# A hybrid encoder layer on one core: gate-times-up blocks turned by VectorE in squares of 32 and moved across partitions by ScalarE, in place of TensorE's transposes; one seven-product pair fewer in each second chunk

## The chip, the cores and the metric

One core of a Trainium2 chip runs the whole layer in one launch. The metric is the device time in microseconds (us), the median of three runs. All engines, queues and times below are those of this one core.

## The reference

Only the two SwiGLU half-steps are touched, the first and the last stage of the layer (the stages between, projections and three branches, are unchanged):

```python
def rmsnorm(x, g):
    y = xf * lax.rsqrt(jnp.mean(xf * xf, axis=-1, keepdims=True) + EPS)
    return y * g

def swiglu(x, w_gate, w_up, w_down):
    return (jax.nn.silu(x @ w_gate) * (x @ w_up)) @ w_down

x = x + 0.5 * swiglu(rmsnorm(x, ffn1_norm), ffn1_w_gate, ffn1_w_up, ffn1_w_down)
...
x = x + 0.5 * swiglu(rmsnorm(x, ffn2_norm), ffn2_w_gate, ffn2_w_up, ffn2_w_down)
```

x has 256 tokens and 2048 columns, the hidden width is 5632, all in float32.

## The kernel before

**Precision.** Every large product is made of three matmuls. An operand is split into a high part (rounded to the type fp32r, by ScalarE) and a low part (what is left, by VectorE): `wh` and `wl` for weights, `lhs[:, 0]` and `lhs[:, 1]` for the left side. The three matmuls are low times high, high times high, and high times low (`product` in `pair_gemm`, and the same in `gemm` and `down_pieces`).

**Tiling of a half-step.** The hidden width is cut into 11 chunks of 512 columns (`HID`). Chunk c computes gate and up together (`pair_gemm`), in 8 steps, the pairs j: each takes two blocks of 128 rows of the input width, for 2 halves of the tokens (t = 0, 1) and the two matrices. A pair is a 2x2 by 2x2 block product and is made either with eight products (24 matmuls of 128x512) or, after Strassen and Winograd, with seven (21 matmuls). A seven-product pair also needs sums of weight blocks: VectorE adds them (`sums`), ScalarE and VectorE split them (`sumsh`, `sumsl`), beside the split of three of the four own blocks (`wh`, `wl` 128x1536). An eight-product pair needs the split of four blocks (128x2048) and nothing else. `SEVEN` holds the pairs that have seven-product operands on the left side, six of eight. Chunk 0 takes no seven-product pair, chunk 1 of the first half-step takes pairs 2, 4 and 6 (`SEVEN[1::2]`), all others take six.

**After a chunk.** The products gather in eight PSUM banks and end in two tiles in SBUF, gate and up, of 128 partitions (tokens) by 2 by 512. They come from a pool of four (`tmp`) and are called `gate`, `up` or, where they are the second set of the chunk, `late_gate`, `late_up`. ScalarE applies silu to the gate, VectorE multiplies (`product` in `up(c)`, a SCALAR_TENSOR_TENSOR on `late_up`). The result is needed turned, with hidden columns on the partitions, as the left operand of the down product. `turned_lhs` does that with TensorE: 8 transposes of 128x128 per chunk (matmuls `bank<-ident,late_up`) into two PSUM banks, and from each bank a split by ScalarE and VectorE (`lhs<-bank`) into the operand `hT[c]`. They are queued as `turns` and run after the last seven-product pair of the next chunk (`after_seven`).

**Down.** The down product of chunk c is cut into 8 pieces of 12 matmuls and spread between the products of chunk c+2 (`down_pieces`, `between`). Each piece ends with a ScalarE copy `y<-down` and a DMA from GpSimd's queue that adds y to x in DRAM. The last two chunks' down products come at the end of the half-step, in `gemm`.

**What sets the order.** All instructions are recorded first. `Plan.issue` then plays them through with assumed costs and writes out one fixed order for each engine: an engine takes, among the instructions whose inputs are there, the one recorded first; `shifted(n)` lets an instruction count as recorded n places later. `queue` and `pop` spread small work between the products. Weights, sums, splits and left operands share 23 places (`slot`) of 8 KB per partition; a weight's DMA waits until a place is free.

Of the kernel before, what the change touches and what calls it, by code (L numbers as in the profile page):

```python
# [13 lines left out]
AF = mybir.ActivationFunctionType  # L14
# [3 lines left out]
P = 128  # L18
S = 256
T = S // P  # L20
# [22 lines left out]
SEVEN = (1, 2, 3, 4, 5, 6)  # L43
SUMS = (220, 400)
HID = DFF // CW
MIXV = (0, 3)
APART = 4
BETWEEN = 4
# [133 lines left out]
class Plan:  # L182
# [36 lines left out]
    def record(self, engine, name, args, kw):  # L219
        values = list(args) + [v for k, v in kw.items() if k not in ("out", "accum_out")]  # L220
        out = kw.get("out")
        if out is None:
            out, values = args[0], values[1:]
        views = [v for v in values if isinstance(v, View)]
        outs = [v for v in (out, kw.get("accum_out")) if isinstance(v, View)]

        def call():
            real = lambda v: v.real() if isinstance(v, View) else v
            return getattr(getattr(self.nc, engine), name)(*map(real, args), **{k: real(v) for k, v in kw.items()})  # L229

        w = Work(engine, call, *self.cost(engine, name, out, views, kw))
        if name == "dma_start":
            side = out if isinstance(out, View) else views[0]
            w.bytes, w.adds = 4 * P * side.free(), "accum_op" in kw
        w.link = LINKS.get(getattr(kw.get("func", args[2] if name == "activation" else None), "name", None), 0)
        before, tiles = set(), {}
        for view, writes in [(v, False) for v in views] + [(v, True) for v in outs]:
            t, bits = view.tile, view.bits()
            tiles[id(t)] = t
            for other, theirs, wrote in t.log:  # L240
                chained = engine == other.engine == "tensor"
                if other is not w and (theirs & bits and (writes or wrote) or chained and writes and wrote):
                    before.add(other)
            if writes:
                t.log = [x for x in t.log if x[1] & ~bits]
            t.log.append((w, bits, writes))
        w.tiles = tuple(tiles.values())
        for t in w.tiles:
            if t.users == 0:
                t.group.tiles.append(t)  # L250
                t.turn = len(self.works) + self.shift
            t.users += 1
        w.waits = len(before)
        for b in before:
            b.then.append(w)
        w.index = len(self.works) + self.shift
        self.works.append(w)
# [159 lines left out]
def tile_encoder_layer(ctx: ExitStack, tc: tile.TileContext, a: dict, out: bass.AP):  # L417
    nc = Plan(tc)
# [15 lines left out]
    def lslot():  # L434
        return slot([P, 2, 4, S], F32R, "lhs")
# [82 lines left out]
    pending = set()  # L518

    def queue(*work, soon=False):  # L520

        later.extend((f, soon) for f in work)
# [253 lines left out]
    def turned_lhs(src, among, gain=None):  # L776
# [14 lines left out]

        return L, [f for half in range(2) for f in turn_steps(src, half, among, then(half))]

    def turned_pairs(places, n, src, gain):

        pieces = []
        turned = {}

        def by_squares(i):
            if i == 0:  # L800
                turned["y"] = tmp([P, 4, S], "turned")
            turn_pieces(turned["y"], src)[i]()

        pieces += [lambda i=i: by_squares(i) for i in range(4)]
        for half in range(2):
            place = places[2 * n + half]
            pending.add(id(place))
            g = gain[:, 2 * half : 2 * half + 2]
            pieces += fill_pair(place, lambda half=half: turned["y"][:, 2 * half : 2 * half + 2], g)
            pieces.append(lambda place=place: pending.discard(id(place)))  # L810
        return pieces
# [63 lines left out]
    lhs1 = pair_tiles()  # L875
# [4 lines left out]
    def load_x(j):  # L880

        if j % 4 == 0 and j:
            xts.append(slot([P, 8, S], F32, "xt"))
        xt = xts[-1][:, 2 * (j % 4) : 2 * (j % 4) + 2]
        step = 1 if j == 0 else 2
        fill = fill_pair(lhs1[j], lambda: xt, g_ffn1[:, 2 * j : 2 * j + 2], SUMS[j not in SEVEN[1::2]], j == 0)

        def part(k):
            if j or k:
                nc.sync.dma_start(out=xt[:, k : k + step], in_=a["xT"][:, 2 * j + k : 2 * j + k + step, :])  # L890
            for f in fill[:1] if step == 1 else fill:
                f()
            del fill[:1]

        return [lambda k=k: part(k) for k in range(0, 2, step)]
# [24 lines left out]
    def ffn(lhs, rstd, w_gate, w_up, w_down, after_chunk, operand=None, first=None, side=()):  # L920

        hT = {}
        turns, held = [], []

        def second(j):

            if j < 2:
                return [lambda q=q: load_rows(q) for q in (2 * j, 2 * j + 1)]
            if j == 3:
                queue(lambda: rstd.append(rstd_of(ssq1)), *held, soon=True)  # L930
            return ()

        def up(c):

            nonlocal turns
            opening = c == 0 and first is not None
            kw = dict(before=first, pieces=lambda j: 1 if j < 2 else 2) if opening else {}
            if c == 1 and first is not None:
                kw = dict(before=second)
            out = []  # L940
            sevens = () if c == 0 else SEVEN[1::2] if c == 1 and first is not None else SEVEN
            order = [j for j in range(KB // 2) if j not in sevens]
            order = range(KB // 2) if c == 0 or kw else [*sevens, *order]
            between = down_pieces(c - 2) if c > 1 else ()
            pair_gemm(lhs, (w_gate, w_up), (c * CW, c * CW), order, sevens, out, turns, between=between, soon=c == HID - 1, **kw)
            g, u = out
            def silu(t):
                nc.scalar.activation(g[:, t], g[:, t], AF.Silu, scale=rstd[0][:, t : t + 1])

            def product(t):  # L950
                nc.vector.scalar_tensor_tensor(
                    u[:, t], u[:, t], rstd[0][:, t : t + 1], g[:, t], op0=ALU.mult, op1=ALU.mult
                )

            done = [lambda t=t, f=f: f(t) for t in range(T) for f in (silu, product)]
            if opening:
                held.extend(done)
            else:
                queue(*done, soon=True)
            hT[c], turns = turned_lhs(u, (0, 1) if c < HID - 1 else (4, 5))  # L960
            if c == HID - 1:
                queue(*turns)

        def down_pieces(c):

            L = hT.pop(c)
            W = {}

            def piece(n, t):
                if t == 0:  # L970
                    W[n] = weights(w_down, c * CW, n * CW)
                b = psum(7, [P, CW], "down")
                wh, wl = W[n]
                for k in range(4):
                    hi = L[:, 0, k, t * P : (t + 1) * P]
                    lo = L[:, 1, k, t * P : (t + 1) * P]
                    nc.tensor.matmul(b, lo, wh[:, k], start=k == 0, stop=False)
                    nc.tensor.matmul(b, hi, wh[:, k], start=False, stop=False)
                    nc.tensor.matmul(b, hi, wl[:, k], start=False, stop=k == 3)
                y = half_tmp([P, CW], F32, "y")  # L980
                nc.scalar.activation(y, b, AF.Copy, scale=0.5)
                nc.gpsimd.dma_start(out=XD[n][t], in_=y, accum_op=ALU.add)

            return [lambda n=n, t=t: piece(n, t) for n in range(NCH) for t in range(T)]

        for c in range(HID):
            up(c)
        operands = [hT.pop(c) for c in (HID - 2, HID - 1)]
        for n in range(NCH):
            if side:  # L990
                queue(*side[n], soon=True)
            xs = x_chunk(n)
            acc = gemm(operands, w_down, (HID - 2) * CW, n * CW, last=n == NCH - 1 and first is None)

            def residual(t, n=n, acc=acc, xs=xs):
                nc.vector.scalar_tensor_tensor(xs[:, t], acc[t], 0.5, xs[:, t], op0=ALU.mult, op1=ALU.add)
                after_chunk(n, t, xs)

            queue(*(lambda t=t, f=residual: f(t) for t in range(T)), soon=True)
            if operand is not None:  # L1000
                operand(n, xs)
# [566 lines left out]
```

## Time and profile before

| | us |
|---|---|
| median of 3 runs (2264.16 to 2264.96) | 2264.72 |
| the profiled execution, its own time | 2264.33 |
| its span, first to last instruction | 2262.6 |
| first half-step, about | 0 to 700 |
| stages between, about | 700 to 1600 |
| second half-step, about | 1600 to 2262 |

GpSimd is busy for 194.8 us, nearly all of it issuing DMAs. The DMA queues moved 525 MB, 232 GB/s over the span. To read the rows below: a row of the page or of a group gives line, engine and operation, out<-in with buffer numbers left out, shapes and count, then busy time and the mean ns of one, then idle time before them and who ended it. A timeline row gives start, duration, engine, operation and count. Almost every row names line 229, the helper that issues what the planner has ordered, so groups are told apart by tile names. A matmul's duration is longer than the time until the next one starts, since matmuls overlap; what one costs is read from starts.

### The profile page before, as it was taken

What the parts mean: (1) busy time and instruction counts of PE and PEld (TensorE: products, weight loads), DVE (VectorE), ACT (ScalarE), POOL (GpSimd) and SP (SyncE); (2) the same over time, 40 slices, a digit from 0 to 9 for tenths busy, and PEclk for the clock granted to TensorE, in tenths of its full rate; (3) what the DMA queues carried; (4) which work ended last, traced back from release to release, by engine and by line L of the source; (5) the groups of instructions that cost most, each with busy time, mean ns of one, the idle gap of its engine ahead of it and who ended that gap; (6) DMA issues with size and microseconds to landing.
All of it is one profiled execution on the core that took longest, in us unless ns stands there. A gap on an engine that the chain in (4) does not pass through costs nothing.

```text
span 2262.6 us, 26505 instructions
## 1 busy us (share of the span) xinstructions
PE 2252.0 (100%) x10106; PEld 1857.4 (82%) x10106; DVE 1929.6 (85%) x1972; ACT 1305.5 (58%) x1313; POOL 194.8 (9%) x257
## 2 busy tenths in 40 slices
PE   9999999999999999999999999999999999999998
PEld 7888888888888888888888888888888888888887
DVE  7999999999989787757778787899899989999985
ACT  8666666666666454443334454455566666666663
POOL 0011111111110000000000000000011111111110
PEclk9999999999999999999999999999999999999999
DMA  9688899988996555565454556665488898988892
GB/s 372 211 242 252 252 259 264 255 241 249 277 334 217 203 204 168 196 213 197 169 195 174 178 208 230 230 214 211 173 250 240 249 262 246 267 245 244 255 321 115
DMA packets 121584, 525.06 MB, mean 232 GB/s; under 512 B 14320, under 2 KB 14576, under 8 KB 90224
## 3 DMA queue, kind: packets, MB, share of 16 engines
q1 hardware_dynamic: 88848, 444.15, 55.6%
q0 software_dynamic: 32176, 78.66, 17.5%
q8 instruction: 79, 1.29, 0.2%
q10 hardware_dynamic: 432, 0.56, 0.1%
q14 instruction: 49, 0.40, 0.1%
HBM read 458.30 MB, written 46.14 MB: 223 GB/s over the span
## 4 chain that ended last, share of the span: by engine, by line
PE 95%; issue 2%; DMA 1%; DVE 1%; POOL 0%; ACT 0%; SPq 0%; DVEq 0%; POOLq 0%; ACTq 0%
PE acc L229 40%; PE q L229 36%; PE down L229 16%; PE bank L229 2%; DMA x<-y 1%; DMA wf<-in_ffn_w_up 1%; DVE wl L229 0%; POOL x L229 0%; ACT wh L229 0%; SPq L229 0%; DVE sums L229 0%; ACT y L229 0%; POOL late_up L229 0%; POOL late_gate L229 0%; DVE up L229 0%
## 5 line engine op out<-in xcount | busy, mean ns | idle before, releaser
L229 DVE TENSOR_TENSOR wl<-wf,wh 128x2048 fp32r<-128x2048 f32 (+2 forms) x422 | 884.3, 2109 | 106.2 <-ACT wh L229 84.0
L229 ACT ACTIVATE wh<-wf 128x2048 fp32r<-128x2048 f32 (+2 forms) x422 | 741.9, 1769 | 305.3 <-DMA wf<-in_w_in 107.2
L229 PE MATMUL acc<-wh,lhs 128*128 128x512 f32 x2688 | 830.3, 390 | 0.0
L229 PEld LDWEIGHTS acc<-wh,lhs 128*128 128x128 f32 x2688 | 502.5, 188 | 102.6
L229 PE MATMUL acc<-wl,lhs 128*128 128x512 f32 x1344 | 522.7, 389 | 0.0
L229 PE MATMUL down<-wh,lhs 128*128 128x512 f32 x1152 | 357.6, 391 | 0.9 <-ACT y L229 0.8
L229 ACT ACTIVATE sumsh<-sums 128x1024 fp32r<-128x1024 f32 x234 | 244.5, 1058 | 128.7 <-DVE sums L229 123.1
L229 DVE TENSOR_TENSOR sumsl<-sums,sumsh 128x2048 fp32r<-128x2048 f32 x117 | 267.7, 2288 | 45.7 <-ACT sumsh L229 44.7
L229 PEld LDWEIGHTS acc<-wl,lhs 128*128 128x128 f32 x1344 | 252.3, 188 | 52.7
L229 PE MATMUL q<-wh,seven 128*128 128x512 f32 x942 | 292.2, 389 | 0.0
L229 PE MATMUL q<-sumsh,seven 128*128 128x512 f32 x936 | 288.0, 389 | 0.0
L229 PEld LDWEIGHTS down<-wh,lhs 128*128 128x128 f32 x1152 | 215.1, 188 | 48.4 <-ACT y L229 4.6
L229 PE MATMUL q<-wh,lhs 128*128 128x512 f32 x704 | 230.5, 407 | 0.1
L229 PE MATMUL down<-wl,lhs 128*128 128x512 f32 x576 | 224.6, 390 | 0.0
L229 PEld LDWEIGHTS q<-wh,seven 128*128 128x128 f32 x942 | 176.8, 188 | 36.7
L229 PEld LDWEIGHTS q<-sumsh,seven 128*128 128x128 f32 x936 | 175.7, 188 | 36.4
L229 POOL DMA_DIRECT2D x<-y x144 | 123.9, 861 | 808.3 <-ACT y L229 754.7
L229 PE MATMUL q<-wl,seven 128*128 128x512 f32 x471 | 182.9, 389 | 0.2 <-DVE wl L229 0.2
L229 ACT ACTIVATE y<-down 128x512 f32<-128x512 f32 x144 | 86.0, 597 | 161.4 <-PE down L229 127.9
L229 PE MATMUL q<-sumsl,seven 128*128 128x512 f32 x468 | 174.9, 389 | 0.0
L229 DVE TENSOR_TENSOR sums<-sums,wf 128x512 f32<-128x512 f32 x234 | 161.9, 692 | 7.9
L229 PEld LDWEIGHTS q<-wh,lhs 128*128 128x128 f32 x704 | 124.2, 189 | 28.1 <-ACT wh L229 1.1
(149 smaller groups left out, 1667.4 us busy)
## 6 DMA issues: line engine op xcount, KB each, us to landing
wf<-in_w_in SPq DMA_DIRECT2D x100, 1024.0 KB, 4.8
wf<-in_ffn_w_down SPq DMA_DIRECT2D x88, 1024.0 KB, 7.8
wf<-in_ffn_w_gate SPq DMA_DIRECT2D x174, 512.0 KB, 5.7
wf<-in_ffn_w_up SPq DMA_DIRECT2D x174, 512.0 KB, 6.8
x<-y POOLq DMA_DIRECT2D x144, 256.0 KB, 6.9
wf<-in_w_mem_kv SPq DMA_DIRECT2D x16, 1024.0 KB, 6.3
wf<-in_w_out SPq DMA_DIRECT2D x16, 1024.0 KB, 5.4
late_gate<-gate POOLq DMA_DIRECT2D x18, 512.0 KB, 5.5
```

Of the source, the lines that this page charges most:

```text
L229: return getattr(getattr(self.nc, engine), name)(*map(real, args), **{k: real(v) for k, v in kw.items()})
```

## The change

1. In all chunks of both half-steps but the last (10 of 11 each), `turned_lhs` is replaced by `moved_lhs`. VectorE turns the 512 columns of one token half in one instruction on all 128 partitions, in squares of 32x32 (`squares`, 2 per chunk), from up into the gate tile, which silu and product no longer need. A square is turned where it stands, so its partition group stays the token's. ScalarE then moves the squares to the partition group of their columns, from the gate tile back into the up tile, in 16 copies of 32 partitions x 256 (`move`), which the planner counts as recorded 200 places later (`MOVED`). The split into `hT[c]` reads the up tile in SBUF (`part`, 2 per chunk) and stands in the place of the old `turns`. The last chunk of each half-step keeps the transposes.
2. `SECOND` replaces the choice for chunk 1: pairs 2 and 4 in the first half-step (before 2, 4, 6), pairs 1 to 5 in the second (before 1 to 6). In the first, `SUMS` also puts the left-side sums of pair 6 later.
3. The planner's size of a DMA counts the partitions that it touches (the same number as before for a tile of 128 partitions).

```diff
+SECOND = ((2, 4), (1, 2, 3, 4, 5))
+MOVED = 200
...
-            w.bytes, w.adds = 4 * P * side.free(), "accum_op" in kw
+            w.bytes, w.adds = 4 * 32 * side.cells.shape[0] * side.free(), "accum_op" in kw
...
+    def moved_lhs(src, spare):
+        L = lslot()
+        pending.add(id(L))
+        w = spare.rearrange("p t c -> p (t c)").rearrange("p (q t k r) -> p q t k r", q=4, t=T, k=4)
+        y = src.rearrange("p t c -> p (t c)").rearrange("p (g t k r) -> p g t k r", g=4, t=T, k=4)
+        def squares(t):
+            to = w[:, :, t].rearrange("p q k r -> p k q r")
+            nc.vector.transpose(to, src[:, t].rearrange("p (k q c) -> p k q c", q=4, c=32))
+        def move(g, q):
+            with nc.shifted(MOVED):
+                nc.scalar.activation(y[32 * q : 32 * q + 32, g], w[32 * g : 32 * g + 32, q], AF.Copy)
+        def part(t):
+            to = [L[:, i, :, t * P : (t + 1) * P].rearrange("p k (g r) -> p k g r", r=32) for i in range(2)]
+            split(*to, y[:, :, t].rearrange("p g k r -> p k g r"))
+            if t == T - 1:
+                pending.discard(id(L))
+        moves = [lambda g=g, q=q: move(g, q) for g in range(4) for q in range(4)]
+        return L, [lambda t=t: squares(t) for t in range(T)] + moves, [lambda t=t: part(t) for t in range(T)]
...
-        fill = fill_pair(lhs1[j], lambda: xt, g_ffn1[:, 2 * j : 2 * j + 2], SUMS[j not in SEVEN[1::2]], j == 0)
+        fill = fill_pair(lhs1[j], lambda: xt, g_ffn1[:, 2 * j : 2 * j + 2], SUMS[j not in SECOND[0]], j == 0)
...
-            sevens = () if c == 0 else SEVEN[1::2] if c == 1 and first is not None else SEVEN
+            sevens = () if c == 0 else SECOND[first is None] if c == 1 else SEVEN
...
+            moves = []
+            if c < HID - 1:
+                hT[c], moves, turns = moved_lhs(u, g)
             if opening:
-                held.extend(done)
+                held.extend(done + moves)
             else:
                 queue(*done, soon=True)
-            hT[c], turns = turned_lhs(u, (0, 1) if c < HID - 1 else (4, 5))
+                queue(*moves)
             if c == HID - 1:
+                hT[c], turns = turned_lhs(u, (4, 5))
                 queue(*turns)
```

The planner lays the order out anew. Three places of one chunk in the middle of the first half-step show it. (A number behind a tile's name only tells tiles apart; the same tile has another number in the two programs.)

TensorE, behind the last seven-product pair, before: `late_up` is the gate-times-up block of the chunk before, `wh`/`wl` the weights of the two eight-product pairs.

```order
L229 MATMUL q_2335<-wh_2618,lhs_100 128x512 x2
L229 MATMUL bank_2656<-ident,late_up_2283 128x128 x2
L229 MATMUL q_2341<-wh_2618,lhs_100 128x512 x2
L229 MATMUL bank_2656<-ident,late_up_2283 128x128 x2
L229 MATMUL q_2347<-wh_2618,lhs_100 128x512
L229 MATMUL down_2669<-wh_2591,lhs_2191 128x512 x2
```

The same place on TensorE now:

```order
L231 MATMUL down_2709<-wh_2641,lhs_2189 128x512 x2
L231 MATMUL down_2709<-wl_2664,lhs_2189 128x512
L231 MATMUL q_2359<-wl_2703,lhs_100 128x512
L231 MATMUL q_2359<-wh_2661,lhs_100 128x512 x2
L231 MATMUL q_2359<-wl_2703,lhs_100 128x512
L231 MATMUL q_2363<-wl_2703,lhs_100 128x512
L231 MATMUL q_2363<-wh_2661,lhs_100 128x512 x2
```

The transposes are gone, and the eight-product matmuls stand next to each other and to the down piece.

VectorE from the product of gate and up on, before:

```order
L229 SCALAR_TENSOR_TENSOR late_up_2283<-late_up_2283,rstd_618,late_gate_2263 128x512 x2
L229 TENSOR_TENSOR sumsl_2404<-sums_2359,sumsh_2371 128x2048
L229 TENSOR_TENSOR wl_2424<-wf_2349,wh_2413 128x2048
L229 TENSOR_TENSOR sums_2442<-wf_2378 128x1024
L229 TENSOR_TENSOR sums_2442<-sums_2442,wf_2378 128x512 x2
L229 TENSOR_TENSOR wl_2462<-wf_2378,wh_2431 128x1536
L229 TENSOR_TENSOR sumsl_2477<-sums_2442,sumsh_2451 128x2048
```

and now:

```order
L231 SCALAR_TENSOR_TENSOR late_up_2311<-late_up_2311,rstd_625,late_gate_2288 128x512 x2
L231 STREAM_TRANSPOSE late_gate_2288<-late_up_2311 128x4x4x32 x2
L231 TENSOR_TENSOR sumsl_2446<-sums_2391,sumsh_2400 128x2048
L231 TENSOR_TENSOR wl_2461<-wf_2377,wh_2442 128x2048
L231 TENSOR_TENSOR sums_2478<-wf_2403 128x1024
L231 TENSOR_TENSOR sums_2478<-sums_2478,wf_2403 128x512 x2
L231 TENSOR_TENSOR wl_2499<-wf_2403,wh_2468 128x1536
L231 TENSOR_TENSOR sumsl_2517<-sums_2478,sumsh_2492 128x2048
```

The two transposes stand right behind the product; what follows is the same as before.

ScalarE from the split `wh` 128x2048 behind the silu on, before:

```order
L229 ACTIVATE wh_2413<-wf_2349 128x2048
L229 ACTIVATE wh_2431<-wf_2378 128x1536
L229 ACTIVATE sumsh_2451<-sums_2442 128x1024
L229 ACTIVATE y_2459<-down_2426 128x512
L229 ACTIVATE sumsh_2451<-sums_2442 128x1024
L229 ACTIVATE wh_2474<-wf_2410 128x2048
```

and now:

```order
L231 ACTIVATE wh_2442<-wf_2377 128x2048
L231 ACTIVATE late_up_2311<-late_gate_2288 32x256 x3
L231 ACTIVATE wh_2468<-wf_2403 128x1536
L231 ACTIVATE late_up_2311<-late_gate_2288 32x256 x5
L231 ACTIVATE sumsh_2492<-sums_2478 128x1024
L231 ACTIVATE y_2502<-down_2456 128x512
L231 ACTIVATE sumsh_2492<-sums_2478 128x1024
L231 ACTIVATE wh_2514<-wf_2435 128x2048
```

Eight of the 16 moves stand before and behind one weight split; five, one and two more follow further on, ahead of later `sumsh` and `y` copies of the same chunk.

## The prediction

> **What bounds the kernel now.** I read the page's busy times first, then the waits of TensorE over the whole span, then one chunk of a half-step as a window.
>
> ```profile
> PE 2252.0 (100%) x10106; PEld 1857.4 (82%) x10106; DVE 1929.6 (85%) x1972; ACT 1305.5 (58%) x1313; POOL 194.8 (9%) x257
> ...
> PE idle L229 <- DVE idle L229: 1.3, 1, 1.3
> PE down L229 <- ACT y L229: 0.8, 1, 0.8
> PE q L229 <- DVE wl L229: 0.2, 1, 0.2
> ...
> 268.37:330.68 62.31, 62.31 (x280) 51.23 (x279) 57.01 (x46) 41.06 (x42) 8.61 (x10) 1.00 0.89 254
> ```
>
> TensorE is busy all the time, and a busy share can deceive, since matmul ends are modelled. The waits settle it: in 2262.6 us it waits 2.3 us for others. The window is one chunk, from a VectorE instruction to the same one a chunk later: 62.31 us, no gap on TensorE at the full clock, VectorE busy for 57.01 and ScalarE for 41.06. So the kernel is bound by the number of matmuls in line, and work taken off TensorE is time, as long as VectorE, which is nearly full itself, still delivers weights in time. These are the two questions.
>
> **What goes from TensorE.** The cost of a transpose is read from starts in the timeline, not from its duration.
>
> ```profile
> L229 PE MATMUL bank<-ident,late_up 128*128 128x128 f32 x144 | 33.7, 271 | 0.0
> L229 PE MATMUL bank<-ident,up 128*128 128x128 f32 x32 | 6.4, 272 | 0.0
> ...
> 272.80 0.27 PE L229 MATMUL bank<-ident,late_up 128*128 128x128 f32 x1
> ...
> 273.61 0.27 PE L229 MATMUL bank<-ident,late_up 128*128 128x128 f32 x1
> ...
> 274.41 0.27 PE L229 MATMUL bank<-ident,late_up 128*128 128x128 f32 x1
> ...
> 275.22 0.27 PE L229 MATMUL bank<-ident,late_up 128*128 128x128 f32 x1
> ...
> 276.02 0.62 PE L229 MATMUL q<-wh,lhs 128*128 128x512 f32 x2
> 276.48 0.39 PE L229 MATMUL q<-wl,lhs 128*128 128x512 f32 x1
> 276.71 0.62 PE L229 MATMUL q<-wh,lhs 128*128 128x512 f32 x2
> ```
>
> Between these rows stand three matmuls of 128x512 each time. Three of them with a transpose take 0.80 to 0.81 us (272.80 to 273.61, and on), three without take 0.69 (276.02 to 276.71, so 0.23 each). A transpose thus costs 0.115 to 0.13 us of TensorE's time; I take 0.12. The two groups hold 176 = 22 chunks x 8. The two last chunks keep theirs, so 160 go: 160 x 0.12 = **19.2 us** (18.4 to 20.8). The Trainium skill, page "TensorE: Matmul & The Clock Gate", Part 4, tells of about 275 ns for such a transpose in a kernel's context; by it 44 us would go and the sum would be near 2222. The duration in the row, 271 ns, agrees, but the starts show that most of it lies beside other matmuls; the starts decide, and it gets no chance of its own.
>
> **What comes to TensorE.** One pair in chunk 1 of each half-step goes from 21 matmuls to 24: 2 x 3 x 0.23 = **1.4 us**.
>
> **What comes to VectorE.** A transpose on 128 partitions x 512 columns is not in the trace; the nearest are on 32 partitions.
>
> ```profile
> L229 DVE STREAM_TRANSPOSE qkT<-rot 32x256 f32<-32x256 f32 x96 | 41.9, 436 | 1.4
> L229 DVE STREAM_TRANSPOSE ym<-pm 32x128 f32<-32x128 f32 x64 | 19.4, 302 | 1.0
> ```
>
> 128 more columns cost 134 ns, so 512 columns take 436 + 2 x 134 = 704 ns if the four partition groups go side by side, as in every other VectorE row, and four times that, 2.8 us, if they go one after the other. I take 0.70, so 1.4 us per chunk; 2.8 is kept for a rival. What hides it:
>
> ```profile
> 291.28 1.42 DVE L229 SCALAR_TENSOR_TENSOR late_up<-late_up,rstd,late_gate 128x512 f32<-128x512 f32 x2 [0.48 <-DMA late_up<-up]
> ...
> 303.88 2.29 DVE L229 TENSOR_TENSOR sumsl<-sums,sumsh 128x2048 fp32r<-128x2048 f32 x1 [2.52 <-ACT sumsh L229]
> ...
> 306.72 0.39 PE L229 MATMUL q<-sumsl,seven 128*128 128x512 f32 x1
> ...
> DVE sumsl L229 <- ACT sumsh L229: 2.5, 1, 2.5
> DVE wl L229 <- ACT wh L229: 0.9, 1, 0.9
> DVE lhs L229 <- ACT lhs L229: 0.6, 1, 0.6
> DVE late_up L229 <- DMA late_up<-up: 0.5, 1, 0.5
> DVE v L229 <- ACT wh L229: 0.3, 1, 0.3
> ```
>
> The new transposes stand right behind the row at 291.28. Eleven us later VectorE waits 2.52 us for `sumsh`. The `sumsl` behind that wait ends at 306.17 and TensorE uses it at 306.72: a lead of 0.55 us, thin, but set by the wait and not by VectorE's load. So 1.4 us ahead of it only shorten the wait to 1.1. Over the whole chunk: 62.31 less the five waits of the last rows (4.8) leaves 57.5 occupied; with 1.4 it is 58.9. TensorE's chunk shrinks by 8 x 0.12 to 61.35. That leaves 2.4 us for waits, and the four other waits sum to 2.3. It fits, with nothing over. VectorE's two `lhs` splits stay in number and size and only read another memory; I cost that at nothing.
>
> Where the wait is not there, the transposes come through. In the third chunk of the first half-step it is shorter and 22 us behind the product:
>
> ```profile
> 103.84 1.41 DVE L229 SCALAR_TENSOR_TENSOR late_up<-late_up,rstd,late_gate 128x512 f32<-128x512 f32 x2
> ...
> 127.83 2.29 DVE L229 TENSOR_TENSOR sumsl<-sums,sumsh 128x2048 fp32r<-128x2048 f32 x1 [1.00 <-ACT sumsh L229]
> ```
>
> There 1.4 less a lead of some 0.55 is a stall of 0.85 us. With as much again for all other chunks together I take 1.5 us of new waits on TensorE as an estimate, between 0 and 0.85 in each of 20 chunks, 17 us.
>
> **What goes from VectorE in chunk 1.** The pair that turns from seven to eight products:
>
> ```profile
> L229 DVE TENSOR_TENSOR sums<-wf 128x1024 f32<-128x1024 f32 x117 | 142.6, 1219 | 0.0
> L229 DVE TENSOR_TENSOR sums<-sums,wf 128x512 f32<-128x512 f32 x234 | 161.9, 692 | 7.9
> L229 DVE TENSOR_TENSOR sumsl<-sums,sumsh 128x2048 fp32r<-128x2048 f32 x117 | 267.7, 2288 | 45.7 <-ACT sumsh L229 44.7
> L229 DVE TENSOR_TENSOR wl<-wf,wh 128x1536 fp32r<-128x1536 f32 x117 | 205.0, 1752 | 9.3 <-ACT wh L229 8.6 <-PE q L229 0.6
> ```
>
> 1.22 + 2 x 0.69 + 2.29 + 1.75 = 6.64 us go, and one split of 128x2048 at the same 2.29 comes: 4.35 less, against 1.4 more for chunk 0's transposes. Nothing waits there now that this would free, so I count no gain; it pays for the 1.4 in that chunk. The later place of pair 6's left-side sums I cost at nothing: the pair is then an eight-product one and needs them only a chunk later.
>
> **What comes to ScalarE.** 16 copies of 32 x 256 per chunk, whose form is not in the trace. Nearest are wider copies and one of the same width with a gain.
>
> ```profile
> L229 ACT ACTIVATE sumsh<-sums 128x1024 fp32r<-128x1024 f32 x234 | 244.5, 1058 | 128.7 <-DVE sums L229 123.1 <-issue 4.3
> L229 ACT ACTIVATE wh<-wf 128x512 fp32r<-128x512 f32 x8 | 4.9, 630 | 4.2 <-DMA wf<-in_ffn_w_gate 3.2 <-DMA wf<-in_ffn_w_up 1.0
> L229 ACT ACTIVATE lhs<-bank 128x512 fp32r<-128x512 f32 x48 | 28.6, 598 | 55.2 <-PE bank L229 55.2
> L229 ACT ACTIVATE lhs<-xt,gains 128x256 fp32r<-128x256 f32 x18 | 7.9, 504 | 0.3 <-DMA xt<-in_memT 0.3
> ...
> 294.96 1.49 ACT L229 ACTIVATE wh<-wf 128x1536 fp32r<-128x1536 f32 x1 [1.37 <-DVE sumsl L229]
> 298.33 1.06 ACT L229 ACTIVATE sumsh<-sums 128x1024 fp32r<-128x1024 f32 x1 [1.87 <-DVE sums L229]
> 302.30 0.60 ACT L229 ACTIVATE y<-down 128x512 f32<-128x512 f32 x1 [2.91 <-PE down L229]
> ...
> 309.60 1.07 ACT L229 ACTIVATE sumsh<-sums 128x1024 fp32r<-128x1024 f32 x1 [2.08 <-DVE sums L229]
> ```
>
> (1058 - 630) / 512 is 0.84 ns per element; 256 fewer than 512 give 0.42 us, and the row with a gain bounds it at 0.50. I take 0.42, so 6.7 us per chunk (8.0 at most), and ScalarE goes from 41 to 48 of 61 us. The order puts eight copies between the `wh` ahead of 294.96 and the `y` at 302.30, where ScalarE idles for 1.37 + 1.87 + 2.91 = 6.15 us: 3.4 to 4.0 us fit. Five more stand ahead of the `sumsh` at 309.60, where 2.08 us idle: 2.1 to 2.5 just fit or miss by 0.4. In its line behind them stand `sumsh`, `y` and `wh`; VectorE's `sumsl` and `wl` wait for those, and TensorE for these. This is the second place of the 0 to 17 us above. The two `lhs` splits read SBUF now and not PSUM, 630 against 598 (the second and third row), 0.06 us per chunk: nothing. `part` needs no bank and follows at once behind the seven-product pairs, so nothing on TensorE waits for it. Queues: neither SyncE nor GpSimd issues another DMA, and none is moved past a queue.
>
> **The sum**, from the profiled execution's own 2264.33 us (median of the runs 2264.72; 1.7 us of it lie outside the span): 2264.3 - 19.2 + 1.4 + 1.5 = **2248.0 us**.
>
> **Rivals.** (a) VectorE's thin lead: the transposes or the copies come through in every chunk by 0.2 to 0.85 us, 20 chunks, 4 to 17 us. For it speaks the lead of 0.55 and a sum that leaves 0.1 us over; against it that the wait of 2.52 lies between the transposes and the thin place. Time 2246.5 + 4 to 17 = 2250.5 to 2263.5, middle 2257. (b) Nothing is left of it: copies ahead of `sumsh` and `y` cost a further 0.9 us per chunk, 17.8 / 20, or the weights' DMAs bind; time 2264. Against the DMAs speaks that the chunk's 254 GB/s would only have to be 258, and that the stretch below had 280 with TensorE at 59.85 of 60.
>
> ```profile
> 580.00:640.00 60.00, 59.85 (x265) 48.90 (x264) 54.84 (x44) 40.72 (x41) 8.51 (x10) 1.00 0.95 280
> ```
>
> (c) Slower: the transpose on 128 partitions goes group by group, 2.8 us. Then a chunk holds 57.5 + 5.6 = 63.1 us of VectorE's work alone, 0.8 more than the chunk of now, and 3.1 with the four waits: 16 to 62 us over 20 chunks, 2280 to 2326. It decides from (62.3 - 57.5 - 2.3) / 2 = 1.25 us for a transpose on. The Trainium skill, page "VectorE: DVE Perf Modes", Rules for kernel authors, says to make a 128x128 transpose on TensorE where PSUM will do as its end, which speaks against the change and would give (c) here; no row shows VectorE as the bound yet.
>
> **How the numbers follow.** The sum as forecast 0.68 (2244, with a transpose at 0.13 and the old wait of 0.8 us for `y` gone, to 2252, into the lower part of a); (a) 0.18; (b) 0.08; (c) 0.06. The range takes in the forecast and three quarters of (a), 0.81 in all: 2244 to 2260. What can be told from no change is about 0.2%, 4.5 us either way: faster 0.82 (the forecast and that part of a), same 0.12, slower 0.06.
>
> **What would show it.** The group of 128x4x4x32 transposes with a mean near 0.70 us, that of 32x256 copies near 0.42; a chunk of 61.3 to 61.5 us; TensorE's waits in total below 4 us; VectorE's wait for `sumsh` shorter than 2.5 us. A transpose above 1.25 us, or waits of TensorE for `wl` or `sumsl` that recur in each chunk, would make it wrong.

## The result and the profile after

| | before | after |
|---|---|---|
| median, us | 2264.44 (2263.44 to 2264.96, 4 runs) | 2245.2 (2244.51 to 2245.35, 4 runs) |
| ratio, 95% interval | | 0.9915 (0.9898 to 0.9932) |
| the profiled execution, its own time, us | 2264.33 | 2244.51 |
| span, us | 2262.6 | 2242.8 |

The change makes the kernel 19.2 us faster, 0.85%. The forecast was 2248.0. The page's busy times, all that TensorE waited for, and one chunk of the first half-step as a window (from a `sums` of VectorE to the same one a chunk later):

```profile
PE 2232.1 (100%) x9952; PEld 1846.1 (82%) x9952; DVE 1944.0 (87%) x2004; ACT 1433.2 (64%) x1629; POOL 194.5 (9%) x257
...
PE idle L231 <- DVE idle L231: 1.3, 1, 1.3
PE q L231 <- ACT wh L231: 1.2, 1, 1.2
...
268.62:329.95 61.33, 61.33 (x271) 50.60 (x270) 58.21 (x47) 47.84 (x57) 8.60 (x11) 1.00 0.89 257
```

In this chunk TensorE is still without gaps and at the full clock. The chunk takes 61.33 us in place of 62.31. ScalarE is busy for 6.8 us more in it and VectorE for 1.2. TensorE's listed waits are 2.5 us in the whole span, against 2.3; both lie in the first 9 us, so from there on none is listed. The new operations, in the view of groups (mean ns behind the busy time):

```profile
L231 DVE STREAM_TRANSPOSE late_gate<-late_up 128x512 f32<-128x512 f32 x36 | 23.5, 691 | 0.6
L231 ACT ACTIVATE late_up<-late_gate 32x256 f32<-32x256 f32 x288 | 119.7, 415 | 9.7 <-DVE late_gate L231 4.6 <-ACT wh L231 0.8
L231 ACT ACTIVATE lhs<-late_up 128x512 fp32r<-128x512 f32 x36 | 20.8, 620 | 0.1
```

The form of VectorE's transpose, which no row of before showed, takes 0.69 us, so the four partition groups go side by side; one after the other it would have been 2.8. VectorE's timeline of that chunk, at the places of the rows shown before, and all that VectorE waited for in it:

```profile
291.45 1.30 DVE L231 STREAM_TRANSPOSE late_gate<-late_up 128x512 f32<-128x512 f32 x2
...
301.69 2.29 DVE L231 TENSOR_TENSOR sumsl<-sums,sumsh 128x2048 fp32r<-128x2048 f32 x1 [0.30 <-ACT sumsh L231]
...
310.95 2.29 DVE L231 TENSOR_TENSOR sumsl<-sums,sumsh 128x2048 fp32r<-128x2048 f32 x1 [0.51 <-ACT sumsh L231]
...
DVE late_up L231 <- DMA late_up<-up: 1.4, 1, 1.4
DVE sumsl L231 <- ACT sumsh L231: 0.8, 2, 0.5
DVE wl L231 <- ACT wh L231: 0.4, 1, 0.4
```

The wait of 2.52 us for `sumsh` has become 0.8 in two pieces, which is where the transposes went, while the wait for `late_up` grew from 0.5 to 1.4. VectorE's five waits of 4.8 us in a chunk are 2.6 in all now.

### The profile page after: what moved, and what is told of

The parts are those of the page before. It is cut to its first block, busy times and chain, and to the rows that moved or that the text cites. A ratio compares the mean times of both kernels' runs of the same rounds, so it can differ in the third digit from the quotient of the medians.

```text
span 2242.8 us, 26639 instructions
## 1 busy us (share of the span) xinstructions
PE 2232.1 (100%) x9952; PEld 1846.1 (82%) x9952; DVE 1944.0 (87%) x2004; ACT 1433.2 (64%) x1629; POOL 194.5 (9%) x257
## 4 chain that ended last, share of the span: by engine, by line
PE 99%; DMA 0%; DVE 0%; ACT 0%; SPq 0%; DVEq 0%; issue 0%
PE acc L231 41%; PE q L231 39%; PE down L231 18%; PE bank L231 2%; DMA wf<-in_ffn_w_gate 0%; SPq L231 0%; ACT junk L231 0%; DVE xs L231 0%; DVEq L1594 0%; ACT wh L231 0%; DVE sm L231 0%; DVE xg L231 0%; ACT sm L231 0%
## 5 line engine op out<-in xcount | busy, mean ns | idle before, releaser
L231 PE MATMUL q<-wh,seven 128*128 128x512 f32 x962 | 299.0, 389 | 0.0
L231 DVE TENSOR_TENSOR sumsl<-sums,sumsh 128x2048 fp32r<-128x2048 f32 x115 | 262.4, 2281 | 38.6 <-ACT sumsh L231 37.7
L231 PE MATMUL q<-sumsh,seven 128*128 128x512 f32 x920 | 278.8, 389 | 0.0
L231 PE MATMUL q<-wh,lhs 128*128 128x512 f32 x704 | 214.3, 390 | 1.2 <-ACT wh L231 1.2
L231 PE MATMUL q<-sumsl,seven 128*128 128x512 f32 x460 | 161.7, 389 | 0.0
L231 PEld LDWEIGHTS q<-wh,lhs 128*128 128x128 f32 x704 | 132.1, 188 | 29.6 <-ACT wh L231 2.3
```

## The experiments

Theory A: the time is TensorE's matmuls in line, and what VectorE and ScalarE get is hidden. Rival B: VectorE (and ScalarE, which it waits for) is the hidden bound, and the relief in chunk 1 lets the gain through. C was added when the result of e7 was in: the order that the planner lays out is worth several us by itself. The kernel before, on the chips of the three groups of runs, took 2264.30, 2264.67 and 2264.34 us.

| run | median, us | lowest to highest | ratio to before, 95% interval |
|---|---|---|---|
| e0 the change again | 2244.91 | 2244.35 to 2247.12 | 0.9916 (0.9903 to 0.9930) |
| e1 turning alone, old pairs | 2252.05 | 2249.89 to 2255.50 | 0.9949 (0.9936 to 0.9961) |
| e2 new pairs alone | 2264.50 | 2263.99 to 2266.63 | 1.0002 (0.9993 to 1.0011) |
| e3 TensorE transposes twice | 2283.23 | 2281.86 to 2284.04 | 1.0082 (1.0068 to 1.0096) |
| e4 VectorE transposes twice | 2267.58 | 2265.80 to 2271.72 | 1.0017 (1.0008 to 1.0026) |
| e5 ScalarE copies twice | 2275.77 | 2275.61 to 2276.20 | 1.0050 (1.0037 to 1.0063) |
| e6 copies not put back | 2285.27 | 2280.73 to 2292.11 | 1.0095 (1.0080 to 1.0110) |
| e7 not turned | 2250.36 | 2247.92 to 2254.73 | 0.9942 (0.9930 to 0.9955) |
| e8 not turned, same order | 2248.00 | 2244.41 to 2250.24 | 0.9924 (0.9911 to 0.9936) |
| e9 VectorE transposes twice, same order | 2249.32 | 2248.07 to 2250.20 | 0.9933 (0.9921 to 0.9945) |
| e10 the change, other order | 2244.66 | 2244.34 to 2248.24 | 0.9917 (0.9903 to 0.9930) |
| e11 turning alone, other order | 2249.73 | 2247.94 to 2251.37 | 0.9935 (0.9923 to 0.9947) |

**e0, the change again.**

> The changed kernel once more, on the chip of the other three, as their measure. Both theories expect 19.2 us less than the kernel before (2264.4 to 2245.2), and the same few waits of TensorE (2.5 us in all, 1.3 of them the start).

2244.91 us, 19.4 below before; TensorE waits 1.9 us in all. The measure holds.

**e3: what a TensorE transpose costs.** On the kernel before:

```diff
-            nc.tensor.transpose(state["b"][:, k, t * P : (t + 1) * P], src[:, t, c : c + P], ident)
+            for _ in range(times):
+                nc.tensor.transpose(state["b"][:, k, t * P : (t + 1) * P], src[:, t, c : c + P], ident)
```

> The kernel before with each of the 176 TensorE transposes of the gate-times-up blocks made twice into the same place. A: each costs TensorE 0.12 us, hidden by nothing: 21.1 us slower than before (20.2 to 22.9), 2285. B (part of TensorE's time lies in slack, and the gain of the change was the relief elsewhere): clearly less, 10 us or under.

18.6 us slower, 18.6 / 176 = 0.105 us for each: A, a little under its range. Chunk by chunk the second transpose costs nearly what the first does: from the first matmul of a chunk's gate and up to that of the next, the chunks in the middle of the first half-step take 63.13 to 63.25 us here and 62.20 to 62.32 before, so 0.93 / 8 = 0.116 us, and (62.31 - 61.33) / 8 = 0.12 is what the change took away. The sum is smaller mainly because the last chunk of the second half-step, where TensorE waited for `y` before, did not grow.

**e2 and e1: each part of the change by itself.** e2 is the kernel before with

```diff
+SECOND = ((2, 4), (1, 2, 3, 4, 5))
...
-            sevens = () if c == 0 else SEVEN[1::2] if c == 1 and first is not None else SEVEN
+            sevens = () if c == 0 else SECOND[first is None] if c == 1 else SEVEN
```

> The kernel before with only the new pairs in chunk 1: TensorE's transposes stay. A: 6 matmuls of 0.23 us more, so 1.4 us slower than before, 2265.8; no wait of TensorE goes, since it had 0.2 us of waits for VectorE in all. B: faster than before, by as much as VectorE held TensorE there in ways that the waits do not show, 2262 or less.

0.2 us slower (the interval reaches from 1.6 us faster to 2.5 slower): the times cannot tell A's 1.4 slower from nothing, but they could tell B's 2 us faster, and it is not there. The trace shows A's matmuls: chunk 1 takes 0.74 us more in the first half-step and 0.68 in the second, 1.4 together. Other chunks got shorter by as much, the last one of the second half-step by 0.45, where the wait for `y` fell from 0.8 to 0.3. e1 is the changed kernel with

```diff
-SECOND = ((2, 4), (1, 2, 3, 4, 5))
+SECOND = ((2, 4, 6), (1, 2, 3, 4, 5, 6))
```

> The changed kernel with the old pairs in chunk 1 (2, 4, 6 and 1 to 6): only the turning is changed against before. Theory A (TensorE's matmuls in line are the time, VectorE's additions are hidden): 6 matmuls of 0.23 us fewer than the change, so 1.4 us less than it, 2243.8, as long as VectorE holds in chunk 1; with the stall of 0.85 us that I counted there, 2244.7. Rival B (VectorE is the hidden bound, and the 4.35 us that it is relieved of in chunk 1 let the gain through): slower than the change by up to 2 x (4.35 - 1.4) = 5.9 us, 2248 to 2251, with TensorE waiting for wl or sumsl between 40 and 140 us and between 1660 and 1760 us.

7.1 us slower than the change where A expected 0.5 to 1.4 faster: A fails here, and TensorE waits for `sumsh` near 112, 1664 and 1727 us, in B's windows (B had named `wl` or `sumsl`). But the profiled execution is one of the longer ones, 2255.23 us, 10.9 above that of e0, and 4.8 of these 10.9 us lie between the half-steps, from the last gate-and-up matmul of the first to the first one of the second, which the edit does not touch; 3.4 of them are one wait near 897 us. Is the rest the pairs' or the order's?

**e10 and e11: the same two kernels in another order.** In each,

```diff
-    HAND = 60
+    HAND = 80
```

> The changed kernel with the planner's assumed hand-over between engines at 80 ns, not 60: the same instructions in another order. A: within 2 us of the change. C (the order is worth several us by itself): up to 6 us slower.

> e1 (the old pairs in chunk 1) with the planner's hand-over at 80 ns. B (relief of VectorE in chunk 1 is worth some 4 us, in any order): slower than e10 by 3 to 7 us, with TensorE waiting again in the third chunk of both half-steps, near 112 and 1665 us. C (e1's loss was its order): no more than 2 us from e10, on either side.

e10 is where the change is, so this other order costs nothing and C has no case here; e11 is 5.1 us behind it. The waits in the third chunk of both half-steps are there again, at 110 and 1659 us, so they belong to the pairs: B. The two largest sums among TensorE's waits in e11, and the ScalarE row that stands ahead of the second, in e11 and then in the change:

```profile
PE q L231 <- ACT sumsh L231: 2.9, 4, 1.3
PE bank L231 <- ACT lhs L231: 1.9, 1, 1.9
...
890.61 1.06 ACT L231 ACTIVATE lhs<-pool_w 128x1024 fp32r<-128x1024 f32 x1 [3.49 <-DMA pool_w<-in_pool_w]
```

```profile
887.73 1.06 ACT L231 ACTIVATE lhs<-pool_w 128x1024 fp32r<-128x1024 f32 x1 [1.49 <-DMA pool_w<-in_pool_w]
```

The wait for `lhs` near 895 us hangs on one DMA, `pool_w`, between the half-steps. In e1, e6, e7, e10 and e11 alike TensorE goes on 5.86 or 5.87 us after it has landed. From issue to landing it took 7.8 us in e11 and 9.2 in e1, 6.2 in e10 and 5.8 in the change. The pairs are no likely reason, since it is late in e6 and e7 too (9.7 and 7.4), which have the new ones; what made it late is not shown. Of the 5.1 us between e10 and e11, 2.1 lie between the half-steps and 3.0 in them. The third chunk of the first half-step in e11, ScalarE, VectorE and TensorE:

```profile
106.70 2.99 ACT L231 ACTIVATE late_up<-late_gate 32x256 f32<-32x256 f32 x7 [0.27 <-ACT wh L231]
109.71 1.06 ACT L231 ACTIVATE sumsh<-sums 128x1024 fp32r<-128x1024 f32 x1
...
105.31 1.31 DVE L231 STREAM_TRANSPOSE late_gate<-late_up 128x512 f32<-128x512 f32 x2
106.54 1.72 DVE L231 TENSOR_TENSOR wl<-wf,wh 128x1536 fp32r<-128x1536 f32 x1
108.17 1.22 DVE L231 TENSOR_TENSOR sums<-wf 128x1024 f32<-128x1024 f32 x1
...
109.04 0.84 PE L231 MATMUL q<-wl,seven 128*128 128x512 f32 x3
110.82 1.19 PE L231 MATMUL q<-sumsh,seven 128*128 128x512 f32 x4 [0.94 <-ACT sumsh L231]
112.35 0.97 PE L231 MATMUL q<-sumsh,seven 128*128 128x512 f32 x3 [0.33 <-ACT sumsh L231]
```

TensorE stands for `sumsh`. ScalarE makes it at 109.71 because its seven copies end there, 0.3 us after the `sums` it needs (108.17 + 1.22 = 109.39). VectorE makes those `sums` late because the two transposes stand ahead of them. From starts, TensorE loses 1.10 and 0.62 us there (109.04 to 110.82 less three matmuls of 0.227, 110.82 to 112.35 less four); in the second half-step it loses 1.4 and 0.6 at the same place. VectorE ahead of that place, in e11 and then in the change:

```profile
97.00 1.22 DVE L231 TENSOR_TENSOR sums<-wf 128x1024 f32<-128x1024 f32 x1
...
103.87 1.41 DVE L231 SCALAR_TENSOR_TENSOR late_up<-late_up,rstd,late_gate 128x512 f32<-128x512 f32 x2
```

```profile
93.24 1.22 DVE L231 TENSOR_TENSOR sums<-wf 128x1024 f32<-128x1024 f32 x1
...
99.70 1.22 DVE L231 TENSOR_TENSOR sums<-wf 128x1024 f32<-128x1024 f32 x1
...
103.95 1.41 DVE L231 SCALAR_TENSOR_TENSOR late_up<-late_up,rstd,late_gate 128x512 f32<-128x512 f32 x2
```

The product comes at the same time in both, but with the pair of chunk 1 relieved VectorE has the `sums` of three pairs of the third chunk behind it by then, in e11 of two (in both the first of them was made near 82.6). In e10 and the change TensorE has no wait here.

**e4 and e9: how much room VectorE has.**

```diff
-            nc.vector.transpose(to, src[:, t].rearrange("p (k q c) -> p k q c", q=4, c=32))
+            for _ in range(2):
+                nc.vector.transpose(to, src[:, t].rearrange("p (k q c) -> p k q c", q=4, c=32))
```

> The changed kernel with each VectorE transpose of 128x4x4x32 made twice, so 2 x 0.69 us more of VectorE per chunk, 28 us in all. A chunk of the change takes about 61.3 us and VectorE some 58.8 of it with the transposes, so 60.2 with them doubled: 1.1 us are left. A: mostly hidden, 0 to 6 us slower than the change (2245 to 2251), with waits of TensorE that are small and not in every chunk. B (VectorE at its limit): the whole 1.25 us of each of 20 chunks comes through, 25 us, 2270.

22.7 us slower than the change: by the time, B. But the waits are of another kind than B's. TensorE and ScalarE in e4:

```profile
203.70 0.39 PE L231 MATMUL down<-wl,lhs 128*128 128x512 f32 x1
203.93 0.39 PE L231 MATMUL q<-wh,lhs 128*128 128x512 f32 x1
204.83 0.73 PE L231 MATMUL down<-wh,lhs 128*128 128x512 f32 x2 [0.51 <-ACT y L231]
...
204.18 0.60 ACT L231 ACTIVATE y<-down 128x512 f32<-128x512 f32 x1 [2.12 <-PE down L231]
...
PE down L231 <- ACT y L231: 10.0, 17, 1.8
```

One down piece ends, one other matmul follows, and the next piece waits until ScalarE has copied the first out of the one PSUM bank that all pieces use. From starts that costs 0.67 us (203.93 to 204.83 less one matmul), so 17 such waits are about half of the 22.7. The change has four matmuls there:

```profile
202.18 0.39 PE L231 MATMUL down<-wl,lhs 128*128 128x512 f32 x1
202.41 1.07 PE L231 MATMUL q<-wh,lhs 128*128 128x512 f32 x4
203.32 0.72 PE L231 MATMUL down<-wh,lhs 128*128 128x512 f32 x2
```

The planner, which in e4 knew of the doubled cost, had laid the pieces closer together. So e9 issues the transposes twice without the planner's knowledge, in the change's order (`w.times` is 2 for them):

```diff
             for w in order:
-                w.call()
+                for _ in range(w.times):
+                    w.call()
```

> The changed kernel in its order, with each VectorE transpose issued twice, which the planner does not know: 1.25 us more of VectorE per chunk. A (some 2 us of each chunk are still free on VectorE): 0 to 6 us slower than the change. B (VectorE has nothing left): 20 us or more, as e4. C: between, since in e4 the planner answered the doubled cost with another order, with TensorE waiting for y 0.67 us in each chunk; without that about 10 us less than e4.

4.4 us slower than e0 in place of 22.7: A's number, and C's point, larger than C put it. VectorE is busy for 28 us more than in e0 (1972.3 against 1944.3), and some 23 of them are hidden. The other 18 us of e4 came with the order that the planner laid out for the doubled cost.

**e5: how much room ScalarE has.**

```diff
+                for _ in range(2):
                     nc.scalar.activation(y[32 * q : 32 * q + 32, g], w[32 * g : 32 * g + 32, q], AF.Copy)
```

> The changed kernel with each of ScalarE's 320 copies across partitions made twice: 6.6 us more of ScalarE per chunk, so 54 to 55 of 61 us busy. A (ScalarE has room, its idle time takes copies in): 0 to 5 us slower than the change. B (the copies stand in line ahead of sumsh and y, and VectorE has no time left to wait for them): 0.5 us or more in each of 20 chunks, 10 us or more, 2255 and up.

30.9 us slower than e0: A is wrong, and the size is B's. The planner knew of these copies, so this is room and order together. What TensorE waited for:

```profile
PE q L231 <- ACT wh L231: 5.9, 7, 1.9
PE down L231 <- ACT y L231: 4.3, 9, 1.0
PE down L231 <- DVE wl L231: 4.1, 10, 0.8
PE down L231 <- ACT wh L231: 2.0, 3, 1.1
```

In a window of 62 us (330 to 392) ScalarE is busy for 53.18, so it is not full. What TensorE waits for are splits and `y`, which ScalarE makes in the same line as the copies, and what VectorE makes from them. How much of the loss is room and how much order, no run shows.

**e6: the place of the copies.**

```diff
-MOVED = 200
+MOVED = 0
```

> The changed kernel with MOVED at 0: the planner lets the copies go ahead of everything recorded after them. A (copies are free only where they fill ScalarE's idle time): 16 in a row, 6.6 us, ahead of wh, sumsh and y hold VectorE up once a chunk by 1 to 4 us, of which TensorE's lead takes some: 5 to 40 us slower than the change. B (the place does not matter, there is room): within 2 us of the change.

40.4 us slower than e0, slower than before by 20.6: A, at the upper end of its range. The profiled execution is the longest of the five, 2292.11 us. ScalarE and TensorE in one chunk, and the largest sum among TensorE's waits in the whole span:

```profile
297.82 5.95 ACT L231 ACTIVATE late_up<-late_gate 32x256 f32<-32x256 f32 x14
306.13 0.60 ACT L231 ACTIVATE y<-down 128x512 f32<-128x512 f32 x1 [2.36 <-PE down L231]
...
305.70 0.39 PE L231 MATMUL down<-wl,lhs 128*128 128x512 f32 x1
306.78 0.73 PE L231 MATMUL down<-wh,lhs 128*128 128x512 f32 x2 [0.69 <-ACT y L231]
...
PE down L231 <- ACT y L231: 22.7, 30, 1.7
```

14 copies go in a row, and the largest part of the loss that is listed, 22.7 us of 47.8 in this execution, is again two down pieces with nothing between them: it does not come the way that A said (`wh` and `sumsh` held up), but through the order on TensorE. The rest is not traced.

**e7 and e8: without the turning.** e7 takes both additions out of what the planner sees:

```diff
-        return L, [lambda t=t: squares(t) for t in range(T)] + moves, [lambda t=t: part(t) for t in range(T)]
+        return L, [], [lambda t=t: part(t) for t in range(T)]
```

> The changed kernel without VectorE's transposes and ScalarE's copies in the 20 chunks: the split reads the block as it is, so the down product of these chunks takes an operand that is not turned. A (both are hidden in the change): 2244 to 2245, as the change. B (a part still costs): 2240 or less.

5.5 us slower than e0, with less work: neither theory. Its waits stand in places, not in every chunk:

```profile
PE down L231 <- ACT y L231: 2.9, 2, 1.9
PE acc L231 <- DVE lhs L231: 1.9, 1, 1.9
PE bank L231 <- ACT lhs L231: 1.5, 1, 1.5
...
652.13 1.71 ACT L231 ACTIVATE lhs<-xt,gains 128x256 fp32r<-128x256 f32 x4 [6.80 <-DMA xt<-in_memT]
...
1897.92 1.33 ACT L231 ACTIVATE late_gate<-late_gate,rstd 128x512 f32<-128x512 f32 x2 [5.49 <-DMA late_gate<-gate]
1899.16 0.57 ACT L231 ACTIVATE y<-down 128x512 f32<-128x512 f32 x1
```

The longest of them stand behind DMAs that landed late. One is a `y` that stands in ScalarE's line behind the silu, and the silu behind an adding DMA; these took up to 9.9 us to land in this execution (6.2 at most in the change's). The waits for `acc` and `bank` lie between the half-steps, where nothing of the turning is: the first behind the DMA of `xt` (the row at 652.13; in the change ScalarE waits 3.29 us there), the second behind that of `pool_w`. Of the 9.8 us by which this execution (2254.1 us) is longer than that of e0, 5.5 lie between the half-steps. So e7 does not tell what the turning costs. e8 keeps the change's order and leaves the turning out when it issues (`w.times` is 0 for it).

> The changed kernel in exactly its order, but VectorE's transposes and ScalarE's copies of the 20 chunks are planned and then left out, so the down product of these chunks takes an operand that is not turned. A (both are hidden in the change): within 1 us of the change, 2244 to 2246. C (the order that the planner lays out is worth several us by itself, which would be why e7, with less work, was slower): the same 2244 to 2246, and 5 us below e7. B (a part of the additions still costs): 2241 or less.

The profiled execution took 2244.7 us, with a span of 2243.0 against the change's 2242.8 and 2242.6 and TensorE's waits at 2.1 us: in this execution removing the turning gains nothing, so A. The median, 2248.0, is above what all theories expected, and 2.4 us below e7 and not 5: two of the five executions lie at 2244.4 and 2244.7, three at 2248.0 to 2250.2. None of the longer three has a profile, so what they waited for stays open; late landings as in e7 would do it, but no run shows it.

## Why the prediction was right

- **What bounds the kernel**: right. TensorE's line of matmuls, before and after.
- **What goes from TensorE**, 160 x 0.12 = 19.2: right. The chunk gives 0.98 / 8 = 0.1225 each, 19.6 us; e3 gives 0.105 by its time and 0.116 by its chunks for a second one. The duration of 271 ns would have been more than twice too much.
- **What comes to TensorE**, 1.4 us: right. Chunk 1 of e2 is 1.4 us longer in the two half-steps together.
- **What comes to VectorE**, 0.70 us a transpose: 0.69. It goes into the wait for `sumsh`, as the rows of before showed, and e8 and e9 bear it out: the profiled execution without the transposes, in the same order, gains nothing, and even twice of them costs 4.4 us of 28. So rival (c), with groups one after the other, falls.
- **What comes to ScalarE**, 0.42 us a copy: 0.415, and they fit into its idle time in the order of the change. That this hangs on the place I had only half seen: with the copies at their own place (e6) it costs 40 us, and with twice as many (e5) 31.
- **New waits of 1.5 us**: the mis-sized term, and of the wrong sign. The spans give 2262.6 - 19.2 + 1.4 - 2.0 = 2242.8, so in its place 2.0 us went. TensorE's listed waits grew by 0.2 only, and the last chunk of each half-step became shorter by 1.5 and 2.0 us, 0.5 and 1.0 beyond its eight transposes. In the second half-step that is where TensorE had waited 0.8 us for `y`, which I had put into the lower end of the range. The last half microsecond is spread over the chunks. The reckoning of this term was loose as well: twice 0.85 is 1.7 and not 1.5.
- **Chunk 1's pairs**: here the step failed. "Nothing waits there now that this would free, so I count no gain; it pays for the 1.4 in that chunk." Nothing waited in the kernel before, and alone the edit is indeed worth nothing (e2, 0.2 us slower). With the turning it is worth 3.0 us in the half-steps (e10, e11) to 6.0 (e0, e1). The stall in the third chunk that I had counted at 0.85 us, as left over with the edit in, is 1.7 and 2.0 us in the two half-steps without the edit, with more waits behind it, and with the edit there is none. It also stands at another place than I had put it: not at the `sumsl` of 127.83, where a wait of 1.00 us would have taken most of it, but some 7 us behind the start of the product, at the `sumsh` that TensorE needs at 110.82 in e11. I had seen a stall and the relief and not put them together. Rival (a), the thin lead, is what turning alone does in these places; the edit takes it away. That the sum still came within 3 us has some luck in it: a stall that was not there was counted, and the relief that removes it was not.

## What to carry to other kernels

When one engine bounds a kernel and has no gaps, work moved off it is worth what the starts around it show, not its duration. That holds if the engine that takes the work has waits at the right place, and if the copies are put where their queue idles: the same 16 copies a chunk cost nothing that can be seen when they count 200 places later, and 40 us at their own place. Judge two edits together: one that frees an engine which nothing waits for was worth nothing alone, and 3 to 6 us beside one that loads it. Before a load experiment is read as "the engine is full", run it with the order held fixed, since a planner's answer to a doubled cost (18 of 23 us here) is not the engine's. And before a loss is put down to an edit, look whether it lies in the stage that the edit touches: 4.8 of 10.9 us in e1 did not.

## What the hardware showed unexpectedly

After one gap of TensorE of 1.92 us in e7, eight matmuls of 128x512 started about 0.43 us apart in place of 0.23, and the granted clock of that stretch was 0.81; another gap, of 1.94 us, was followed by none of this. The two stretches as windows (clock in the third column from the end):

```profile
653.00:662.00 9.00, 7.08 (x24) 5.53 (x24) 5.11 (x8) 5.41 (x7) 0.00 (x0) 0.81 0.45 178
...
1896.00:1904.00 8.00, 6.06 (x27) 4.68 (x26) 4.58 (x6) 6.08 (x8) 1.08 (x2) 1.00 0.96 258
```

Gaps of 1.89 us (e11) and 1.91 (e5) were followed by none of it either, while after the gap of 3.24 us in e1 the granted clock was 0.89 (892 to 908 us). What tells the gap of 1.92 us from the others, no run here shows.

ScalarE's copies of 32 partitions do not overlap, while other ScalarE instructions do. In the change's timeline five take 2.13 us, 0.43 each, while the `sumsh` at 300.61 starts 0.1 us before the `y` ahead of it has ended:

```profile
295.67 2.13 ACT L231 ACTIVATE late_up<-late_gate 32x256 f32<-32x256 f32 x5
...
300.12 0.60 ACT L231 ACTIVATE y<-down 128x512 f32<-128x512 f32 x1 [0.69 <-PE down L231]
300.61 1.05 ACT L231 ACTIVATE sumsh<-sums 128x1024 fp32r<-128x1024 f32 x1
```
